# A streaming-encoder trunk on one core: the work beside the convolution's first block in another order

## The chip, the cores and the metric

The kernel runs on one core of a Trainium2 chip, as one program. The metric is its time on the device in microseconds (us), the median of several executions. PE is TensorE, DVE VectorE, ACT ScalarE, POOL GpSimd, SP SyncE, which here does nothing but start DMAs. Each engine takes its own instructions strictly in the order in which the program gives them to it, and waits for another engine's result where it needs one.

## The reference

Two layers work on 256 tokens of width 2048. The first mixes tokens with a convolution module, the second with latent attention, each followed by a squared-ReLU MLP; the edit lies in the convolution module and the norm ahead of it.

```python
def rms_norm(x, g):
    y = x * lax.rsqrt(jnp.mean(x * x, axis=-1, keepdims=True) + 1e-6)
    return y * g

def conv_module(h, w_pw1, b_pw1, w_dw, b_dw, ln_g, ln_b, w_pw2, b_pw2):
    u = h @ w_pw1 + b_pw1                     # 2048 -> 4096
    a, gate = jnp.split(u, 2, axis=-1)
    u = a * jax.nn.sigmoid(gate)
    u = lax.conv_general_dilated(u, w_dw, padding=[(30, 0)], ...) + b_dw   # 31 taps per channel
    u = jax.nn.silu(layer_norm(u, ln_g, ln_b))
    return u @ w_pw2 + b_pw2

x = x + conv_module(rms_norm(x, norm_mixer_g[0]), ...)
```

## The kernel before

Channels lie on the 128 partitions: h transposed is 16 chunks k of 128 channels by 256 tokens. The product with `w_pw1` and the convolution go through 16 blocks c of 128 channels. A block's product has two halves, the value and the gate, each a sum over the 16 chunks in a PSUM bank (`pss[c]`).

**The head.** Until the row sums of x are known, the norm's factor r isn't either. So x arrives in column parts, PE turns it chunk by chunk (`turn0`, L1048), and `gained(k)` takes the turned chunk from PSUM to `xg`, times the gain g (ACT L1053, DVE L1055). Block 0 is multiplied as plain fp32 from `xg`, without r (`first_products`, L1064). Then `rsqrt` gives r, PE turns it into a row (L1117), ACT copies that to SBUF (L1121), and for each pair p of chunks (8 pairs) three steps prepare the other blocks: `scaled(p)` multiplies the pair by r (DVE L1133), `upper(p)` rounds it to fp32r (ACT L1136), `lower(p)` subtracts the rounded from the unrounded (DVE L1139). Both parts are in `xt`, four tiles of two pairs each: `xt_96` has pairs 0 and 1, `xt_99` pairs 6 and 7. Block 0 gets its r behind the product, by two multiplications from PSUM (DVE L859).

**The weights.** A load n is 8 chunks of 256 columns (1 MB, in two DMAs of 512 KB, `conv_load`); load 2c + 0 or 1 belongs to block c. `conv_half(n, h)` splits one half of a load: ACT rounds (`hi`, L170), and GpSimd subtracts (`lo`, L174, 128x1024) for all loads of this stage. `conv_mm` (L837) then makes three products for each chunk and half: hi with upper, hi with lower, lo with upper. Block 1 reads load 2 with pairs 0 to 3, and load 3 with pairs 4 to 7.

**A block's round.** In round c, `glu(c - 1)` computes the sigmoid of the gate on ACT (`sg`, L861), the value plus its bias on ACT (`vb`, L870), and their product `ub`, on GpSimd (L871); for the last two blocks DVE does the latter two in one operation. `start_sum` begins two sums in PSUM with the first taps (ACT L901); one tap more is made on ACT for GpSimd (L876). `dve_taps` adds the others on DVE, one operation each (L931: `ub` from SBUF, the sum from PSUM), with the end of one block interleaved with the start of the next. PE meanwhile does `conv_mm(c)`, and later turns finished blocks for the layer norm's statistics (`to_tokens`, `ln_stats`), which need all blocks.

The order of the whole head is written out by hand (`manual_schedule`): an engine's order is the order of these calls in the program. Small vectors that the stage needs come as rows through seven DMAs on SP's queue (`stage_rows`, L307), and PE turns them (L312), as it turns the taps' weights (L1162), from where DVE copies them (L1165, L1166). In round 1 the pairs 6 and 7 are scaled, rounded and subtracted between `glu(0)` and the rounding of load 3's second half.

Of the kernel before, what the change touches and what calls it, by code (L numbers as in the profile page):

```python
# [10 lines left out]
F32 = mybir.dt.float32  # L11
# [3 lines left out]
AF = mybir.ActivationFunctionType  # L15
# [64 lines left out]
def trunk_kernel(  # L80
# [59 lines left out]
    def nm(s):  # L140
        uid[0] += 1
        return f"{s}_{uid[0]}"
# [615 lines left out]
    with ExitStack() as cx:  # L758
# [89 lines left out]
        def sum2_tile():  # L848
            return psum["sum"].tile([P, NB], F32, tag="sum2", name=nm("sum2"), bufs=1)

        def glu(c):
            ub = ubs[c] = branches[c % 3]
            sg = cv2.tile([P, S], F32, tag="sg", name=nm("sg"), bufs=1)
            va, ga = pss.pop(c)
            if c == 0:

                vb = cv2.tile([P, S], F32, tag="vb", name=nm("vb"), bufs=1)
                for o, ps in ((sg, ga), (vb, va)):
                    nc.vector.tensor_tensor(o, ps[:, :S], b2[:, :S], op=ALU.mult)  # L859
                va, ga = vb, sg  # L860
            nc.scalar.activation(sg, ga[:, :S], AF.Sigmoid, bias=b_pw1[:, KC + c : KC + c + 1])  # L861
            if c in (KC - 2, KC - 1):

                nc.vector.scalar_tensor_tensor(
                    out=ub[:, PAD:], in0=va[:, :S], scalar=b_pw1[:, c : c + 1], in1=sg, op0=ALU.add, op1=ALU.mult
                )
            else:
                if c > 0:
                    vb = cv2.tile([P, S], F32, tag="vb", name=nm("vb"), bufs=1)
                nc.scalar.activation(vb, va[:, :S], AF.Identity, bias=b_pw1[:, c : c + 1])  # L870
                nc.gpsimd.tensor_tensor(ub[:, PAD:], vb, sg, op=ALU.mult)  # L871

# [142 lines left out]
        with tc.manual_schedule():  # L1015
# [17 lines left out]
            def block_stats(n):  # L1033
                nc.vector.bn_stats(xst[:, n, :], xs[:, 0, n * NB : (n + 1) * NB])
# [11 lines left out]
            def turn0(ks, t):  # L1046
                for k in ks:
                    nc.tensor.transpose(where[k][:, t * P : (t + 1) * P], xs[:, t, k * P : (k + 1) * P], ident)  # L1048

            def gained(k, eng=nc.scalar):  # L1050
                g = g_mix[0][:, k : k + 1]
                if eng is nc.scalar:
                    nc.scalar.activation(xg[:, k, :], where[k], AF.Copy, scale=g)  # L1053
                else:
                    nc.vector.tensor_scalar(xg[:, k, :], where[k], scalar1=g, scalar2=None, op0=ALU.mult)  # L1055

            def first_products(*ks):


                order = [(k, b) for k in ks for b in range(2)]  # L1060
                if ks[-1] == KC - 1:
                    order.sort(key=lambda r: -r[1])
                for k, b in order:
                    nc.tensor.matmul(  # L1064
                        pss[0][b][:, :S], raws[k // 8][:, k % 8, b * P : (b + 1) * P], xg[:, k, :],
                        start=k == 0, stop=k == KC - 1,
                    )
# [12 lines left out]
            pss[0] = [acc_tile() for _ in range(2)]  # L1080

            gained(0)
            block_stats(2)
# [10 lines left out]
            turn0(range(8, 12), 1)  # L1094
            for p, tile_ in ((6, tr_tile), (7, sum_tile)):
                bank(p, tile_())
            turn0(range(12, 16), 0)
            first_products(2)
            turn0(range(12, 16), 1)
            first_products(3)  # L1100
# [10 lines left out]
            gained(4)  # L1111
            gained(5)
            for k in (6, 7):
                gained(k, nc.vector)
# [6 lines left out]
            nc.scalar.activation(r_row, r_ps[:, :S], AF.Copy)  # L1121
# [6 lines left out]
            def part(p, i):  # L1128
                return xt[p // 2][:, p % 2 * 2 : p % 2 * 2 + 2, i * S : (i + 1) * S]

            def scaled(p):
                row = r_row.rearrange("p (a n) -> p a n", a=1).broadcast_to([P, 2, S])
                nc.vector.tensor_tensor(pair(xr, p), pair(xg, p), row, op=ALU.mult)  # L1133

            def upper(p):
                nc.scalar.activation(part(p, 0), pair(xr, p), AF.Copy)  # L1136

            def lower(p):
                nc.vector.tensor_tensor(part(p, 1), pair(xr, p), part(p, 0).bitcast(F32), op=ALU.subtract)  # L1139

            first_products(4, 5)
            scaled(0)
            upper(0)
            for p in range(4):
                for k in (8 + 2 * p, 9 + 2 * p):
                    gained(k)
                scaled(p + 1)
                upper(p + 1)
                lower(p)
                first_products(6 + 2 * p, 7 + 2 * p)  # L1150
                if p == 0:
                    conv_load(3)
                if p in (1, 3):
                    conv_half(2, p // 2)
            scaled(5)
            upper(5)
            warm(AF.Sigmoid)
            lower(4)
            vt, wt = sum2_tile(), tr_tile()
            turn(n_vecs2, vecs2_rows, vt)  # L1160
            for j in range(4):
                nc.tensor.transpose(wt[:, j * NW : (j + 1) * NW], w_rows[j][:NW, :], ident[:NW, :NW])  # L1162
            first_products(14, 15)
            lower(5)
            nc.vector.tensor_copy(vecs[:, n_vecs:], vt[:, :n_vecs2])  # L1165
            nc.vector.tensor_copy(w_dw, wt[:, : 4 * NW])  # L1166
            conv_load(4)
            for c in range(1, KC + 1):
                n = UC * c
                conv_load(n + 3)  # L1170
                if c == 4:
                    nc.sync.dma_start(b2, conv_b_pw2[0:1, :].partition_broadcast(P))
                    nc.scalar.dma_start(pos_i, positions[0].rearrange("(t p) -> p t", p=P))
                    nc.scalar.dma_start(fr, inv_freq[0:1, :].partition_broadcast(P))
                glu(c - 1)
                if c == 1:
                    for p in (6, 7):
                        scaled(p)
                        upper(p)
                    conv_half(3, 0)  # L1180
                    for p in (6, 7):
                        lower(p)
# [791 lines left out]
```

## Time and profile before

| | us |
|---|---|
| median of 3 runs | 1937.01 |
| lowest and highest | 1936.37, 1937.33 |
| profiled execution | 1938.44 |
| span of its profile | 1936.7 |
| mean granted TensorE clock | 0.998 |
| PE, DVE, ACT, POOL busy | 1921.3, 1593.7, 1095.4, 240.9 |

A row of the timeline gives the start of an operation and its length in us, then engine, line, operation, the tiles written and read, partitions by elements, and how many are joined in the row; in brackets stands the idle time of the engine ahead of it and whose end came last before it began. In a row of windows, each engine has its busy time within the stretch and the number of its instructions. In the chain of waits each row is a piece of the time to the end, put down to what ran or was waited for.

### The profile page before, as it was taken

The numbers are of one execution on the slowest core, as the hardware profiler recorded it, in microseconds if no ns is written. First come the engines' busy times: TensorE is split into PE (matmuls) and PEld (weight loads), VectorE is DVE, ScalarE is ACT, GpSimd is POOL, SyncE is SP. The second block draws the span as 40 slices with busy tenths as digits, with TensorE's granted clock in tenths as the row PEclk, the third lists the DMA queues.
The fourth block names the chain that finished last, engine by engine and source line by source line (L and its number), as shares of the span: only waits on it lengthen the run. The fifth ranks groups of instructions, "written<-read, shape, count | busy, mean of one in ns | idle before, by whom it ended". The sixth has DMA issues, their size and how long they took to land.

```text
span 1936.7 us, 28367 instructions
## 1 busy us (share of the span) xinstructions
PE 1921.3 (99%) x10673; PEld 1680.6 (87%) x10673; DVE 1593.7 (82%) x2450; ACT 1095.4 (57%) x1643; POOL 240.9 (12%) x205
## 2 busy tenths in 40 slices
PE   8999999999999999999999999999999999999998
PEld 7999888888888888888898998888888888888886
DVE  6999989867999776799976765877789987778897
ACT  5557755555555555555576655555555554455554
POOL 4999200000010100000001420000000010000000
PEclk9999999999999999999999999999999999999999
DMA  7666456656576866546556445565546776665774
GB/s 224 197 190 181 154 194 213 186 189 196 173 235 211 250 196 196 187 171 204 204 180 185 141 132 184 164 212 184 191 160 224 218 248 220 193 195 175 231 221 145
DMA packets 230458, 375.48 MB, mean 194 GB/s; under 512 B 16424, under 2 KB 107824, under 8 KB 230064
## 3 DMA queue, kind: packets, MB, share of 16 engines
q1 hardware_dynamic: 224672, 363.28, 58.4%
q0 software_dynamic: 4320, 7.87, 2.2%
q10 hardware_dynamic: 1328, 2.52, 0.4%
q8 instruction: 83, 1.36, 0.3%
q14 instruction: 55, 0.45, 0.1%
HBM read 363.68 MB, written 2.10 MB: 189 GB/s over the span
## 4 chain that ended last, share of the span: by engine, by line
PE 96%; DVE 2%; DMA 1%; ACT 0%; issue 0%; SPq 0%; POOL 0%; ACTq 0%; DVEq 0%
PE acc L655 24%; PE acc L205 15%; PE acc L204 15%; PE acc L203 15%; PE acc L656 13%; PE acc L837 7%; PE acc L1317 2%; DVE sum L931 1%; PE acc L1565 0%; DMA raw<-in_conv_w_pw 0%; PE acc L1596 0%; PE acc L1595 0%; PE acc L1594 0%; PE acc L1566 0%; PE acc L1567 0%; DMA xs<-in_x 0%
## 5 line engine op out<-in xcount | busy, mean ns | idle before, releaser
L174 DVE TENSOR_TENSOR lo<-raw,hi 128x1024 fp32r<-128x1024 f32 (+2 forms) x509 | 602.0, 1197 | 231.5 <-ACT hi L170 224.7
L170 ACT ACTIVATE hi<-raw 128x1024 fp32r<-128x1024 f32 (+2 forms) x570 | 579.7, 1035 | 363.2 <-PE acc L655 203.0
L655 PE MATMUL acc<-xt,hi 128*128 128x512 f32 x2048 | 710.6, 390 | 0.0
L656 PE MATMUL acc<-xt,lo 128*128 128x256 f32 x2048 | 577.5, 282 | 0.0
L655 PEld LDWEIGHTS acc<-xt,hi 128*128 128x128 f32 x2048 | 384.5, 188 | 80.7
L656 PEld LDWEIGHTS acc<-xt,lo 128*128 128x128 f32 x2048 | 387.1, 189 | 0.2
L497 ACT ACTIVATE hi<-raw 128x1024 fp32r<-128x1024 f32 x248 | 228.6, 948 | 230.3 <-DVE raw L505 133.4
L498 DVE TENSOR_TENSOR lo<-raw,hi 128x1024 fp32r<-128x1024 f32 x248 | 263.9, 1087 | 29.4 <-ACT hi L497 25.2
L203 PE MATMUL acc<-hi,sh 128*128 128x512 f32 x514 | 200.1, 389 | 0.0
L205 PE MATMUL acc<-lo,sh 128*128 128x512 f32 x514 | 200.0, 389 | 0.0
L203 PE MATMUL acc<-hi,gh 128*128 128x512 f32 (+1 forms) x516 | 200.0, 388 | 0.0
L205 PE MATMUL acc<-lo,gh 128*128 128x512 f32 (+1 forms) x516 | 199.9, 387 | 0.0
L204 PE MATMUL acc<-hi,gl 128*128 128x512 f32 (+1 forms) x516 | 199.9, 387 | 0.0
L204 PE MATMUL acc<-hi,sl 128*128 128x512 f32 x450 | 175.1, 389 | 0.0
L837 PE MATMUL acc<-xt,hi 128*128 128x256 f32 x960 | 171.7, 282 | 0.3 <-ACT hi L170 0.3
L578 POOL DMA_DIRECT2D xs<-v x30 | 26.4, 976 | 1137.7 <-DVE lo L174 703.3
L931 DVE SCALAR_TENSOR_TENSOR sum<-ub,w_dw,sum 128x256 f32<-128x256 f32 x409 | 164.1, 482 | 2.7 <-ACT sum L901 2.2
L174 POOL TENSOR_TENSOR lo<-raw,hi 128x1024 fp32r<-128x1024 f32 x61 | 145.8, 2410 | 27.3 <-DMA stage<-in_conv_b_dw 20.6
L837 PEld LDWEIGHTS acc<-xt,hi 128*128 128x128 f32 x960 | 147.4, 190 | 0.6 <-ACT hi L170 0.5
L837 PE MATMUL acc<-xt,lo 128*128 128x256 f32 x480 | 134.8, 281 | 1.9 <-POOL lo L174 1.9
L203 PEld LDWEIGHTS acc<-hi,gh 128*128 128x128 f32 x516 | 96.9, 188 | 19.9
L204 PEld LDWEIGHTS acc<-hi,gl 128*128 128x128 f32 x516 | 96.9, 188 | 19.8
(313 smaller groups left out, 2555.0 us busy)
## 6 DMA issues: line engine op xcount, KB each, us to landing
raw<-in_mlp_w SPq DMA_DIRECT2D x255, 1024.0 KB, 5.4
raw<-in_conv_w_pw SPq DMA_DIRECT2D x62, 512.0 KB, 5.1
raw<-in_conv_w_pw SPq DMA_DIRECT2D x16, 1024.0 KB, 5.0
raw<-in_mla_w_o SPq DMA_DIRECT2D x16, 1024.0 KB, 5.3
raw<-in_mla_w_kv_up SPq DMA_DIRECT2D x32, 256.0 KB, 3.8
xs<-v POOLq DMA_DIRECT2D x30, 256.0 KB, 7.8
raw<-in_mla_w_in SPq DMA_DIRECT2D x8, 576.0 KB, 3.7
raw<-in_mla_w_in SPq DMA_DIRECT2D x4, 1024.0 KB
```

Source lines behind the costliest of these rows:

```text
L170: nc.scalar.activation(hi, raw[:, js, :], AF.Copy)
L174: eng.tensor_tensor(lo, raw, hi.bitcast(F32), op=ALU.subtract)
L203: nc.tensor.matmul(ps, sh, mh, start=start, stop=False)
L204: nc.tensor.matmul(ps, sl, mh, start=False, stop=False)
L205: nc.tensor.matmul(ps, sh, ml, start=False, stop=stop)
L497: nc.scalar.activation(hi, src, AF.Copy)
L498: nc.vector.tensor_tensor(lo, src, hi.bitcast(F32), op=ALU.subtract)
L655: nc.tensor.matmul(ps[b], wh[:, bs], xhl(k), start=k == 0, stop=False)
L656: nc.tensor.matmul(ps[b][:, :S], wl[:, bs], xh(k), start=False, stop=k == KC - 1)
L837: nc.tensor.matmul(pss[c][b][:, :S], w[i][:, bs], (xh, xl)[j](k), start=k == i + j == 0, stop=end and k == k0 + nk - 1 and (i, j) == terms ...
L931: nc.vector.scalar_tensor_tensor(out=out, in0=ubs[c][:, w : w + S], scalar=tap(c, w), in1=base, op0=ALU.mult, op1=ALU.add)
L1317: nc.tensor.matmul(ps2[b][t], x_kt(k, t), w[:, bs], start=k == g == i == 0, stop=k == KC - 1 and i == len(group) - 1,)
```

## The change

Five things are done, all in the head and in rounds 1 and the `glu` of block 0.

- PE: products of chunks 0 and 1 come ahead of the turns of chunks 8 to 11 of token half 0, product 2 ahead of the turns of half 1, product 3 ahead of the last turns. Later products also move up in the text, past scalings and splits, which on PE's own order changes nothing.
- `scaled(0)` reads r from PSUM, the copy comes behind it. `scaled(5)` and `scaled(6)` are done by GpSimd. Gains 10 and 13 go to DVE, 6 and 7 to ACT.
- The split of load 2 (both halves) comes behind the copy `upper(4)`; before, its halves stood behind `upper(2)` and `upper(4)`.
- `ub` of block 0 is made by DVE in one operation from `vb`, its bias and `sg`; ACT's `vb` and GpSimd's product go. `lower(5)` comes between the multiplications L859 and this product.
- `upper` and `lower` of pairs 6 and 7 go from ahead of load 3's first half and the sums to behind the sums and load 3's second half, directly ahead of the taps.

```diff
-        def glu(c):
+        def glu(c, between=None):
...
             nc.scalar.activation(sg, ga[:, :S], AF.Sigmoid, bias=b_pw1[:, KC + c : KC + c + 1])
-            if c in (KC - 2, KC - 1):
+            if c == 0:
+                between()
+            if c in (0, KC - 2, KC - 1):
                 nc.vector.scalar_tensor_tensor(
                     out=ub[:, PAD:], in0=va[:, :S], scalar=b_pw1[:, c : c + 1], in1=sg, op0=ALU.add, op1=ALU.mult
                 )
...
+            first_products(0, 1)
+            block_stats(2)
             turn0(range(8, 12), 0)
-            first_products(0, 1)
+            first_products(2)
             block_stats(3)
...
-            def scaled(p):
-                row = r_row.rearrange("p (a n) -> p a n", a=1).broadcast_to([P, 2, S])
-                nc.vector.tensor_tensor(pair(xr, p), pair(xg, p), row, op=ALU.mult)
+            def scaled(p, eng=nc.vector):
+                row = (r_ps[:, :S] if p == 0 else r_row).rearrange("p (a n) -> p a n", a=1).broadcast_to([P, 2, S])
+                eng.tensor_tensor(pair(xr, p), pair(xg, p), row, op=ALU.mult)
...
+            scaled(0)
+            nc.scalar.activation(r_row, r_ps[:, :S], AF.Copy)
...
+            scaled(2)
+            upper(1)
+            scaled(5, nc.gpsimd)
+            first_products(8, 9)
+            lower(1)
...
+            scaled(3)
+            upper(2)
+            scaled(6, nc.gpsimd)
...
+            scaled(4)
+            upper(3)
+            lower(3)
+            upper(4)
+            first_products(12, 13)
             vt, wt = sum2_tile(), tr_tile()
             turn(n_vecs2, vecs2_rows, vt)
...
+            lower(4)
+            conv_half(2, 0)
+            conv_half(2, 1)
+            scaled(7)
+            upper(5)
+            warm(AF.Sigmoid)
             first_products(14, 15)
-            lower(5)
...
-                glu(c - 1)
+                glu(c - 1, lambda: lower(5))
                 if c == 1:
-                    for p in (6, 7):
-                        scaled(p)
-                        upper(p)
                     conv_half(3, 0)
-                    for p in (6, 7):
-                        lower(p)
...
                 side_sum(c - 1)
+                if c == 1:
+                    for p in (6, 7):
+                        upper(p)
+                        lower(p)
                 dve_taps(c - 1)
```

DVE's order from the subtractions of pairs 4 and 5 to the first taps. A number behind a tile's name is its buffer; `ub_129` is the block that the taps read. Before:

```order
L1133 TENSOR_TENSOR xn<-xg,b_125 128x512
L1139 TENSOR_TENSOR xt_98<-xn,xt_98 128x2x256 x2
L1165 COPY vecs<-sum_40_332 128x120
L1166 COPY w_dw<-tr_333 128x496
L859 TENSOR_TENSOR sg_352<-acc_208,b_125 128x256
L859 TENSOR_TENSOR vb_353<-acc_207,b_125 128x256
L1133 TENSOR_TENSOR xn<-xg,b_125 128x512 x2
L1139 TENSOR_TENSOR xt_99<-xn,xt_99 128x2x256 x2
L931 SCALAR_TENSOR_TENSOR sum_371<-ub_129,w_dw,sum_371 128x256
```

DVE's order in the same place now:

```order
L1138 TENSOR_TENSOR xt_98<-xn,xt_98 128x2x256
L1132 TENSOR_TENSOR xn<-xg,b_125 128x512
L1182 COPY vecs<-sum_35_321 128x120
L1183 COPY w_dw<-tr_322 128x496
L859 TENSOR_TENSOR sg_353<-acc_208,b_125 128x256
L859 TENSOR_TENSOR vb_354<-acc_207,b_125 128x256
L1138 TENSOR_TENSOR xt_98<-xn,xt_98 128x2x256
L866 SCALAR_TENSOR_TENSOR ub_129<-vb_354,vecs,sg_353 128x256
L1138 TENSOR_TENSOR xt_99<-xn,xt_99 128x2x256 x2
L932 SCALAR_TENSOR_TENSOR sum_366<-ub_129,w_dw,sum_366 128x256
```

The second subtraction into `xt_98`, `lower(5)`, now stands behind the two multiplications L859; `ub` follows it on DVE, and the scalings of pairs 6 and 7 are gone from between.

GpSimd's order from its first work on data to block 1's `ub` (`ub_130`). Before:

```order
L174 TENSOR_TENSOR lo_302<-raw_140,hi_301 128x1024
L174 TENSOR_TENSOR lo_324<-raw_140,hi_323 128x1024
L871 TENSOR_TENSOR ub_129<-vb_353,sg_352 128x256
L174 TENSOR_TENSOR lo_364<-raw_289,hi_363 128x1024
L174 TENSOR_TENSOR lo_378<-raw_289,hi_377 128x1024
L174 TENSOR_TENSOR lo_457<-raw_346,hi_456 128x1024
L174 TENSOR_TENSOR lo_461<-raw_346,hi_460 128x1024
L871 TENSOR_TENSOR ub_130<-vb_517,sg_515 128x256
```

GpSimd's order now:

```order
L1132 TENSOR_TENSOR xn<-xg,b_125 128x512 x2
L174 TENSOR_TENSOR lo_330<-raw_140,hi_329 128x1024
L174 TENSOR_TENSOR lo_334<-raw_140,hi_333 128x1024
L174 TENSOR_TENSOR lo_361<-raw_287,hi_360 128x1024
L174 TENSOR_TENSOR lo_373<-raw_287,hi_372 128x1024
L174 TENSOR_TENSOR lo_456<-raw_347,hi_455 128x1024
L174 TENSOR_TENSOR lo_460<-raw_347,hi_459 128x1024
L872 TENSOR_TENSOR ub_130<-vb_516,sg_514 128x256
```

Two scalings came ahead of the splits, and the product for block 0 left from between them.

ACT's order from the copy of pair 4 on. Before:

```order
L1136 ACTIVATE xt_98<-xn 128x2x256
L170 ACTIVATE hi_323<-raw_140 128x1024
L1136 ACTIVATE xt_98<-xn 128x2x256
L244 ACT_TABLE_LOAD
L244 ACTIVATE warm_329<-ident 128x1
L861 ACTIVATE sg_352<-sg_352,vecs 128x256
L870 ACTIVATE vb_353<-vb_353,vecs 128x256
L1136 ACTIVATE xt_99<-xn 128x2x256 x2
L170 ACTIVATE hi_363<-raw_289 128x1024
L901 ACTIVATE sum_371<-ub_129,vecs,w_dw 128x256
L901 ACTIVATE sum_51_372<-ub_129,w_dw 128x256
L876 ACTIVATE tp_375<-ub_129,w_dw 128x256
```

ACT's order now, from the two halves of load 2 on:

```order
L170 ACTIVATE hi_329<-raw_140 128x1024
L170 ACTIVATE hi_333<-raw_140 128x1024
L1135 ACTIVATE xt_98<-xn 128x2x256
L244 ACT_TABLE_LOAD
L244 ACTIVATE warm_339<-ident 128x1
L861 ACTIVATE sg_353<-sg_353,vecs 128x256
L170 ACTIVATE hi_360<-raw_287 128x1024
L902 ACTIVATE sum_366<-ub_129,vecs,w_dw 128x256
L902 ACTIVATE sum_51_367<-ub_129,w_dw 128x256
L877 ACTIVATE tp_370<-ub_129,w_dw 128x256
L170 ACTIVATE hi_372<-raw_287 128x1024
L1135 ACTIVATE xt_99<-xn 128x2x256 x2
```

Both roundings of load 2 now stand together behind the copy of pair 4, and the copies of pairs 6 and 7 (`xt_99`) have gone from ahead of load 3 and the sums to behind them.

More of the change, by code (lines that the diff above doesn't have):

```diff
@@ L867, in glu @@
             else:
-                if c > 0:
-                    vb = cv2.tile([P, S], F32, tag="vb", name=nm("vb"), bufs=1)
+                vb = cv2.tile([P, S], F32, tag="vb", name=nm("vb"), bufs=1)
                 nc.scalar.activation(vb, va[:, :S], AF.Identity, bias=b_pw1[:, c : c + 1])
@@ L1082, in trunk_kernel @@
             gained(0)
-            block_stats(2)
             gained(1, nc.vector)
@@ L1094, in trunk_kernel @@
             turn0(range(8, 12), 1)
+            for k in (4, 5, 6):
+                gained(k)
             for p, tile_ in ((6, tr_tile), (7, sum_tile)):
@@ L1097, in trunk_kernel @@
             turn0(range(12, 16), 0)
-            first_products(2)
+            first_products(3)
             turn0(range(12, 16), 1)
-            first_products(3)
             nc.vector.tensor_tensor(xsq[:, 0:1], xsq[:, 0:1], xsq[:, 2:3], op=ALU.add)
@@ L1110, in trunk_kernel @@
             r0 = rsqrt(ms0, T, EPS, "n")
[L1111 to L1114, printed above, removed]
+            gained(7)
             r_ps = sum_tile()
@@ L1120, in trunk_kernel @@
             r_row = b2[:, :S]
-            nc.scalar.activation(r_row, r_ps[:, :S], AF.Copy)
             vecs2_rows = stage_rows(cv, vec_rows2, nc.sync)
@@ L1139, in lower @@
                 nc.vector.tensor_tensor(part(p, 1), pair(xr, p), part(p, 0).bitcast(F32), op=ALU.subtract)
+            scaled(0)
+            nc.scalar.activation(r_row, r_ps[:, :S], AF.Copy)
+            gained(8)
+            gained(9)
             first_products(4, 5)
-            scaled(0)
+            scaled(1)
             upper(0)
[L1144 to L1148, printed above, removed]
-                lower(p)
[L1150 to L1158, printed above, removed]
+            first_products(6, 7)
+            conv_load(3)
+            lower(0)
+            gained(10, nc.vector)
+            gained(11)
+            scaled(2)
[3 more added lines that the diff above has]
+            lower(1)
+            gained(13, nc.vector)
+            gained(12)
+            scaled(3)
+            upper(2)
+            scaled(6, nc.gpsimd)
+            first_products(10, 11)
+            lower(2)
+            gained(14)
+            gained(15)
+            scaled(4)
[3 more added lines that the diff above has]
+            first_products(12, 13)
             vt, wt = sum2_tile(), tr_tile()
@@ L1174, in trunk_kernel @@
                     nc.scalar.dma_start(fr, inv_freq[0:1, :].partition_broadcast(P))
-                glu(c - 1)
+                glu(c - 1, lambda: lower(5))
                 if c == 1:
-                    for p in (6, 7):
-                        scaled(p)
-                        upper(p)
                     conv_half(3, 0)
-                    for p in (6, 7):
-                        lower(p)
                 if c == KC:
```

## The prediction, made before the changed kernel ran

> **What bounds the kernel now.** I read the page first, then the chain of waits, then the head engine by engine.
>
> ```profile
> PE 1921.3 (99%) x10673; PEld 1680.6 (87%) x10673; DVE 1593.7 (82%) x2450; ACT 1095.4 (57%) x1643; POOL 240.9 (12%) x205
> PE 96%; DVE 2%; DMA 1%; ACT 0%; issue 0%; SPq 0%; POOL 0%; ACTq 0%; DVEq 0%
> ```
>
> TensorE is the bound of the kernel as a whole, but the edit touches only the head and the first block of the convolution, so the stage decides. Its windows (columns: PE, PEld, DVE, ACT, POOL busy, granted clock, DMA share, GB/s) and the end of its chain:
>
> ```profile
> 36.00:40.00 4.00, 4.00 (x23) 4.00 (x23) 4.00 (x11) 1.39 (x2) 4.00 (x2) 0.57 0.17 50
> 45.00:60.00 15.00, 15.00 (x131) 15.00 (x130) 15.00 (x39) 9.68 (x14) 14.72 (x9) 1.00 0.69 200
> 60.00:204.00 144.00, 144.00 (x1233) 143.72 (x1233) 143.18 (x365) 93.48 (x179) 137.28 (x78) 1.00 0.64 191
> 204.00:212.00 8.00, 7.67 (x42) 6.57 (x41) 7.76 (x24) 6.22 (x17) 4.67 (x7) 1.00 0.01 2
> ...
> 174.28 5.62 PE acc L837 x48
> 181.91 3.29 DVE sum L931 x9
> 203.77 4.47 DVE sum L931 x12
> 208.48 0.42 DVE ca L939
> ```
>
> From 45 us PE and DVE are both full: DVE's taps (L931) and PE's blocks (L837) keep the same pace, and the last 30 us of the stage's chain are DVE. From 45 to 212 DVE leaves 0.82 + 0.24 = 1.06 us empty. So the stage's end follows the start of the taps, less that 1.06 and less what DVE idles before 45. DVE there:
>
> ```profile
> 23.31 1.71 DVE L1139 TENSOR_TENSOR xt<-xn,xt 128x512 fp32r<-128x512 f32 x1 [2.80 <-ACT xt L1136]
> 24.95 0.68 DVE L1133 TENSOR_TENSOR xn<-xg,b 128x512 f32<-128x512 f32 x1
> 25.55 3.46 DVE L1139 TENSOR_TENSOR xt<-xn,xt 128x512 fp32r<-128x512 f32 x2
> 30.04 0.41 DVE L859 TENSOR_TENSOR vb<-acc,b 128x256 f32<-128x256 f32 x1
> 31.81 1.59 DVE L1139 TENSOR_TENSOR xt<-xn,xt 128x512 fp32r<-128x512 f32 x2 [0.16 <-ACT xt L1136]
> 33.75 8.72 DVE L931 SCALAR_TENSOR_TENSOR sum<-ub,w_dw,sum 128x256 f32<-128x256 f32 x22 [0.35 <-ACT sum L901]
> 44.98 1.27 DVE L931 SCALAR_TENSOR_TENSOR sum<-ub,w_dw,sum 128x256 f32<-128x256 f32 x3 [1.59 <-ACT sum L901]
> ```
>
> The taps begin at 33.75 and stop once, for 1.59 us, before 44.98. GpSimd beside them:
>
> ```profile
> 22.12 2.35 POOL L174 TENSOR_TENSOR lo<-raw,hi 128x1024 fp32r<-128x1024 f32 x1 [20.56 <-DMA stage<-in_conv_b_dw]
> 25.55 2.91 POOL L174 TENSOR_TENSOR lo<-raw,hi 128x1024 fp32r<-128x1024 f32 x1 [1.08 <-ACT hi L170]
> 31.13 1.12 POOL L871 TENSOR_TENSOR ub<-vb,sg 128x256 f32<-128x256 f32 x1 [2.68 <-ACT vb L870]
> 33.34 9.39 POOL L174 TENSOR_TENSOR lo<-raw,hi 128x1024 fp32r<-128x1024 f32 x4 [1.09 <-ACT hi L170]
> ```
>
> **The two exclude each other.** A subtraction L1139 costs about 0.69 us, ends of neighbours 0.6 apart; at 23.31 it took 1.71 and ended at 25.02, just behind GpSimd's split (22.12 + 2.35 = 24.47). At 25.55 DVE had two back to back: the first passed, GpSimd's split, asked for at the same moment, was stretched from 2.35 to 2.91, and the second subtraction ended at 29.01, behind the split's 28.46. So a DVE operation with both operands in SBUF and a GpSimd one hold each other up whole, and the one that waits goes next, even ahead of a back-to-back successor. Taps, with one operand in PSUM, run beside four splits at 33.34 (9.39/4 = 2.35 each) untouched.
>
> **PE in the head.**
>
> ```profile
> 9.23 0.66 PE L1048 MATMUL acc<-ident,xs 128*128 128x128 f32 x4 [1.17 <-DMA xs<-in_x]
> 22.45 1.99 PE L1064 MATMUL acc<-xg,raw 128*128 128x256 f32 x8 [0.66 <-ACT xg L1053]
> 24.96 0.29 PE L312 MATMUL sum<-ident,stage 120*128 120x120 f32 x1 [0.52 <-PE acc L1064]
> 25.52 1.90 PE L1064 MATMUL acc<-xg,raw 128*128 128x256 f32 x8
> 33.32 0.51 PE L837 MATMUL acc<-xt,hi 128*128 128x256 f32 x2 [0.31 <-ACT hi L170]
> 35.76 0.39 PE L837 MATMUL acc<-xt,lo 128*128 128x256 f32 x1 [1.93 <-POOL lo L174]
> ...
> 22.48 0.27 SPq L307 DMA_DIRECT2D stage<-in_mla_kv_norm_g x1
> ...
> L312 PEldq EVENT_SEMAPHORE  x4: 51/51/51, 24.4 to 24.9; - x4
> ```
>
> **The change part by part.**
>
> Products ahead of turns. This attacks the idle 1.17, 0.66 and 0.52. But the turn L312 needs the vector rows; the last is issued at 22.48, PE's sequencer works off its four waits until 24.9, and SP's order and issue times don't move. I keep L312 at 24.96; what PE wins ahead becomes idle there, about 2 us (the three sum to 2.35), worth 0. Bounds: if PE wasn't waiting for those rows, L312 comes up to 1.9 us sooner; if the clock is lowered behind that idle, products 14 and 15 (25.52 to 27.42) take longer. After the only idle of that size, 0.31 + 1.93 just before 35.76, the granted clock was 0.57.
> The Trainium skill (TensorE: Matmul & The Clock Gate, section "Why this matters for your kernels") allows gaps of up to about 3 us before the clock drops. The 0.57 above, behind 1.93 us, disagrees with it, so the measurement decides; by the page alone products 14 and 15 stay at full clock and the early case below gains weight, with its time of 1939.7.
>
> Scalings.
>
> ```profile
> 15.33 1.29 DVE L1133 TENSOR_TENSOR xn<-xg,b 128x512 f32<-128x512 f32 x2 [1.39 <-ACT b L1121]
> ```
>
> The first reads PSUM instead of waiting for ACT's copy of r; of the 1.39 that can give DVE about a microsecond. Pieces 5 and 6 on GpSimd cost there, by an estimate between a 128x256 product (1.12 with a wait in it) and 128x1024 (2.35), 1.3 each, and each holds up the subtraction that DVE asks for meanwhile by up to 1.3; I take 0.7. These cancel within some tenths: range -0.6 to +0.6 on what follows, by ACT's copies.
>
> Weights' split behind copies. ACT's rows:
>
> ```profile
> 23.89 0.64 ACT L1136 ACTIVATE xt<-xn 128x512 fp32r<-128x512 f32 x1
> 33.17 0.55 ACT L901 ACTIVATE sum<-ub,vecs,w_dw 128x256 f32<-128x256 f32 x1
> 34.46 2.93 ACT L170 ACTIVATE hi<-raw 128x1024 fp32r<-128x1024 f32 x3
> 43.06 0.47 ACT L870 ACTIVATE vb<-acc,vecs 128x256 f32<-128x256 f32 x1 [0.93 <-PE acc L837]
> ```
>
> Both halves of n=2 now come behind the copy of piece 4, here at 23.89. Kept there, the rounding starts at 24.5, takes 0.95 (three in 2.93), and GpSimd's two splits run about 25.5 to 27.9 and 27.9 to 30.2, the first copy perhaps some tenths earlier. Before, the first had passed by 24.47. PE's block 1 asks for the first at 27.06: up to 0.8 us of idle, hidden because DVE is later still.
>
> Now DVE. L859 reads block 0 when its last product ends, 27.42, and gives vb by about 27.8. Behind it on DVE stands lower(5), and behind that the product ub (now on DVE, both operands in SBUF), two more subtractions and all taps. lower(5) asks at 27.7 to 27.8, within 0.2 us of the moment at which GpSimd passes from one split to the next. With products 14 and 15 a little late, or the copies a little early, it misses. I take the miss:
> lower(5) waits to 30.2 and ends 30.9; GpSimd's third split, waiting, takes 30.8 to 33.1; ub is done at 33.4. Before it was 31.13 + 1.12 = 32.25.
>
> Then the sums L901 (33.40), the product for GpSimd and the rounding of n=3's second half on ACT, which in the rows above go from 33.17 to 34.46 and on by 0.98: 1.29 + 0.95, so ACT reaches the copy of piece 6 at 35.65. Before, copies 6 and 7 and both subtractions stood ahead of the sums, under no split. Now GpSimd starts its fourth split at 35.7, ahead of lower(6), which asks at 36.2 and gets through at 38.0 to 38.6. The fifth split, waiting, takes 38.6 to 40.85; lower(7) follows and the taps start at 35.7 + 2.3 + 0.55 + 2.3 + 0.55 = **41.4, 7.65 later**. ub itself is hidden there: the sums are ready at 34.4, the taps stand behind lower(7).
>
> PE's block 1 needs lower(6) and lower(7) for its last eighths, so it idles about 1 to 2 us twice near 38.5 and 41; in exchange its old idle 0.31 + 1.93 and its slow stretch go. Its end, at 43.06 before by ACT's wait, stays near 43, ahead of DVE: no further cost. If that cover went, up to 2 us.
>
> Sum: 7.65, less the 1.59 idle that has no reason left, less the 1.06 of slack (all of it, since a late DVE is what the rounds then wait for): +5.0; with no slack recovered +6.1. After the stage all is PE's chain, moved as a whole. The profiled execution (span 1936.7) would become 1941.7; it stands at 1938.44 with what lies around it, the median of the runs at 1937.01. I add to the median: **1942.0**.
>
> **The rivals.**
>
> Early: lower(5) asks in time and passes at 27.9 between the first two splits. For it: 0.2 us either way, and an earlier L312. Then ub waits once (to 31.05) and the rest repeats 2.33 sooner: taps at 39.07, 5.3 late, end +5.3 - 1.59 - 1.06 = +2.7, so 1939.7; with little slack recovered +3.7.
>
> DVE first: it keeps its place with lower(6) and lower(7) back to back. Against it: 25.55, where GpSimd went between two. For it: that is one instance. Saves 2.3: 39.1 after the miss, 36.8 after the early pass; +2.7 to +0.5, so about 1938.5.
>
> No waiting (the other side): the subtractions meet no split, since splits start later than I place them, and the order does what it says. Then ub is done at 29.2, ACT copies 6 and 7 by 33, the taps start at 33.3. Gain 0.45 + 1.59, and up to 1.06 of slack: -2.0 to -3.1, about 1935. PE would allow it: its idle of 0.31 + 1.93 goes, and from 36 to 40 it lost 0.43 x 4 = 1.7 by the clock. It decides if three of four meetings are avoided; the four splits from 33.34 to 42.7, back to back and moved by 2 us at most, speak against it.
>
> **How the numbers follow.** Chances: forecast 0.50, early 0.25, DVE first 0.09, no waiting 0.12, something unseen in PE's head that gives more 0.04. This kernel's measurement tells 0.2%, 3.9 us, from no change. Slower takes the forecast and a fifth of early, 0.55; faster needs more than the -3.1 of no waiting, 0.04 of it and the unseen 0.04: 0.08; same is the rest, 0.37. The range goes from 1937.5 (DVE first at its low end, +0.5) to 1944.4: +6.1, and 1.3 more in case the runs, unlike the profiled execution, seldom had the slow clock at 36 us whose loss the change trades in. The forecast's own range is 1941 to 1944.4.
>
> **What would show it.** DVE's taps begin at 41 (39 if early, 33 to 34 if nothing waits); lower(5), ub, lower(6) and lower(7) with spans of 2 to 3 us and ends just behind a GpSimd split; PE idle of about 2 us before L312 and before the last products of block 1; the layer norm's statistics some 5 us later. I am wrong if the subtractions keep 0.69 us beside the splits, if L312 moves forward by over a microsecond, or if DVE shows idle between 45 and 204 that lets a late start be made up.

## The result, and the profile after

| | median, us | lowest to highest | executions |
|---|---|---|---|
| before | 1936.32 | 1935.62 to 1938.16 | 9 |
| the change | 1941.26 | 1940.39 to 1942.58 | 9 |

The ratio is 1.0025, 95% interval 1.0014 to 1.0035: the change is slower, by 2.7 to 6.8 us. In the profiled execution (1941.32, span 1939.5) the chain of waits, by engine and by line, reads:

```profile
PE 89%; DVE 10%; ACT 1%; issue 1%; DMA 0%; DVEq 0%; ACTq 0%
PE acc L655 24%; PE acc L205 15%; PE acc L203 15%; PE acc L204 15%; PE acc L656 13%; DVE sum L932 8%; PE acc L1333 2%; PE acc L1581 0%; PE acc L1610 0%; PE acc L1612 0%; PE acc L1583 0%; PE acc L1582 0%; PE acc L1611 0%; PE tr L267 0%; PE a
```

Before, PE had 96% and DVE 2%. The convolution's blocks on PE (L837, 7% before) are gone from the chain; in their place stand 8% of DVE's taps (L932, L931 before). So the stage is now DVE's from the first tap to the last. The timeline of DVE:

```profile
27.35 1.41 DVE L1138 TENSOR_TENSOR xt<-xn,xt 128x512 fp32r<-128x512 f32 x1
29.04 2.27 DVE L866 SCALAR_TENSOR_TENSOR ub<-vb,vecs,sg 128x256 f32<-128x256 f32 x1 [0.28 <-ACT sg L861]
34.25 5.26 DVE L1138 TENSOR_TENSOR xt<-xn,xt 128x512 fp32r<-128x512 f32 x2 [2.94 <-ACT xt L1135]
39.43 8.71 DVE L932 SCALAR_TENSOR_TENSOR sum<-ub,w_dw,sum 128x256 f32<-128x256 f32 x22
...
214.22 0.49 DVE L1252 BATCH_NORM_AGGREGATE mv<-stats 128x2 f32<-128x33 f32 x2
```

lower(5) took 1.41, ub 2.27, lower(6) and lower(7) 5.26 together, where a subtraction alone takes 0.69. The taps start at 39.43. GpSimd in the same time, one row for the first scaling and two for six splits back to back:

```profile
18.73 1.27 POOL L1132 TENSOR_TENSOR xn<-xg,b 128x512 f32<-128x512 f32 x1 [17.16 <-ACT xg L1054]
25.70 7.89 POOL L174 TENSOR_TENSOR lo<-raw,hi 128x1024 fp32r<-128x1024 f32 x3 [2.90 <-ACT hi L170]
33.78 7.99 POOL L174 TENSOR_TENSOR lo<-raw,hi 128x1024 fp32r<-128x1024 f32 x3 [0.19 <-ACT hi L170]
```

But for 0.19 us, GpSimd runs without a pause from 25.70 to 41.8, and each of the four DVE operations named above, all with two operands in SBUF, falls into that time. PE, and SP's last vector row:

```profile
21.05 0.29 SPq L307 DMA_DIRECT2D stage<-in_mla_kv_norm_g  x1
...
23.33 0.27 PE L312 MATMUL sum<-ident,stage 120*128 120x120 f32 x1
23.86 1.90 PE L1065 MATMUL acc<-xg,raw 128*128 128x256 f32 x8
28.27 0.39 PE L837 MATMUL acc<-xt,lo 128*128 128x256 f32 x1 [2.10 <-POOL lo L174]
39.56 0.38 PE L837 MATMUL acc<-xt,hi 128*128 128x256 f32 x1 [1.79 <-DVE xt L1138]
```

The turn L312 came 1.6 us sooner than in the profile of before: SP issued the row 1.4 sooner, with SP's order unchanged, and PE didn't have to wait for it. What PE won went into 2.10 us of waiting for the first split. The windows (columns as before the change):

```profile
36.00:40.00 4.00, 2.21 (x17) 1.90 (x16) 4.00 (x4) 0.64 (x1) 4.00 (x3) 1.00 0.61 174
45.00:60.00 15.00, 12.62 (x106) 12.21 (x105) 14.96 (x40) 6.23 (x10) 10.82 (x7) 1.00 0.42 121
60.00:204.00 144.00, 144.00 (x1236) 143.93 (x1235) 143.72 (x369) 97.69 (x182) 137.18 (x79) 1.00 0.65 191
```

DVE has 0.04 + 0.28 us empty from 45 to 204, against 0.82 before: it sets the pace, and PE (12.62 of 15) waits for it.

### The profile page after: what moved, and what is told of

Same layout as the page of the kernel before. It is cut to its first block, busy times and chain, and to the rows that moved or that the text cites. A ratio compares the mean times of both kernels' runs of the same rounds, so it can differ in the third digit from the quotient of the medians.

```text
span 1939.5 us, 28369 instructions
## 1 busy us (share of the span) xinstructions
PE 1921.7 (99%) x10673; PEld 1680.2 (87%) x10673; DVE 1596.6 (82%) x2449; ACT 1095.4 (56%) x1642; POOL 243.5 (13%) x206
## 3 DMA queue, kind: packets, MB, share of 16 engines
q8 instruction: 83, 1.36, 0.3%
## 4 chain that ended last, share of the span: by engine, by line
PE 89%; DVE 10%; ACT 1%; issue 1%; DMA 0%; DVEq 0%; ACTq 0%
PE acc L655 24%; PE acc L205 15%; PE acc L203 15%; PE acc L204 15%; PE acc L656 13%; DVE sum L932 8%; PE acc L1333 2%; PE acc L1581 0%; PE acc L1610 0%; PE acc L1612 0%; PE acc L1583 0%; PE acc L1582 0%; PE acc L1611 0%; PE tr L267 0%; PE acc L1725 0%
## 5 line engine op out<-in xcount | busy, mean ns | idle before, releaser
L204 PE MATMUL acc<-hi,sl 128*128 128x512 f32 x450 | 175.1, 389 | 0.0
L837 PE MATMUL acc<-xt,hi 128*128 128x256 f32 x960 | 170.7, 281 | 2.2 <-DVE xt L1138 1.8
L932 DVE SCALAR_TENSOR_TENSOR sum<-ub,w_dw,sum 128x256 f32<-128x256 f32 x409 | 163.4, 485 | 0.3 <-ACT sum L902 0.2
L837 PEld LDWEIGHTS acc<-xt,hi 128*128 128x128 f32 x960 | 146.2, 188 | 3.0 <-DVE xt L1138 2.0
L837 PE MATMUL acc<-xt,lo 128*128 128x256 f32 x480 | 134.4, 280 | 4.1 <-POOL lo L174 4.1
L205 PEld LDWEIGHTS acc<-lo,sh 128*128 128x128 f32 x514 | 96.5, 188 | 20.6 <-DVE lo L498 0.4
```

The lines of the kernel that those rows point to most:

```text
L204: nc.tensor.matmul(ps, sl, mh, start=False, stop=False)
L205: nc.tensor.matmul(ps, sh, ml, start=False, stop=stop)
L837: nc.tensor.matmul(pss[c][b][:, :S], w[i][:, bs], (xh, xl)[j](k), start=k == i + j == 0, stop=end and k == k0 + nk - 1 and (i, j) == terms ...
L932: nc.vector.scalar_tensor_tensor(out=out, in0=ubs[c][:, w : w + S], scalar=tap(c, w), in1=base, op0=ALU.mult, op1=ALU.add)
```

## The experiments

Each was timed with the kernel before on the same chip. For each profile, the start of the first tap and of the layer norm's aggregation `mv` behind the last one (L1236 before) come from DVE's timeline; their difference is the stage as DVE sees it.

| kernel | median, us | ratio, interval | first tap | mv | difference |
|---|---|---|---|---|---|
| before, first profile | 1936.32 | | 33.75 | 211.65 | 177.90 |
| e1 before again | 1937.16 | 1.0001, 0.9992 to 1.0009 | 32.15 | 210.05 | 177.90 |
| the change | 1941.26 | 1.0025, 1.0014 to 1.0035 | 39.43 | 214.22 | 174.79 |
| e2 pairs back | 1939.53 | 1.0011, 1.0002 to 1.0020 | 37.36 | 212.13 | 174.77 |
| e3 split back | 1941.31 | 1.0023, 1.0014 to 1.0032 | 39.98 | 214.75 | 174.77 |
| e4 ub back | 1941.97 | 1.0025, 1.0015 to 1.0036 | 39.45 | 214.94 | 175.49 |
| e5 before, pairs late | 1941.35 | 1.0019, 1.0011 to 1.0028 | 38.89 | 213.84 | 174.95 |
| e6 pairs first | 1937.62 | 1.0002, 0.9993 to 1.0011 | 36.62 | 212.44 | 175.82 |
| e7 two splits on DVE | 1940.47 | 1.0019, 1.0011 to 1.0028 | 37.35 | 212.80 | 175.45 |
| e8 before, products first | 1937.13 | 1.0000, 0.9991 to 1.0009 | 32.34 | 210.25 | 177.91 |
| e9 scalings back | 1941.04 | 1.0020, 1.0012 to 1.0029 | 38.55 | 213.34 | 174.79 |
| e10 before, splits apart | 1933.96 | 0.9988, 0.9979 to 0.9997 | 32.01 | 206.78 | 174.77 |
| e11 before, third split on DVE, late | 1935.73 | 0.9995, 0.9986 to 1.0004 | 34.56 | 209.69 | 175.13 |
| e12 before, third split on DVE | 1934.87 | 0.9990, 0.9981 to 0.9999 | 32.92 | 207.99 | 175.07 |

The last column is 174.8 to 175.0 in the six profiles whose chain of waits runs through DVE's taps (the change, e2, e3, e5, e9, e10). In the other eight the chain runs for most of the stage through PE's blocks (L837), and the column is larger: 175.1 to 175.8, and 177.9 in the three where DVE waits before the second block's taps. So the stage ends with the later of two paths, the taps' start plus 174.8 or PE's blocks. In before it is PE's; the chain there goes from GpSimd's third split straight into block 1 on PE:

```profile
33.34 2.37 POOL lo L174
...
35.76 24.00 PE acc L837 x190
```

**e1: before again.** No edit.

> The kernel before, unchanged, profiled once more. Its nine runs have a median of 1936.3, the profiled one took 1938.4. Theory clock: the profiled execution paid 1.5 to 1.7 us for the slow clock behind PE's idle at 33.8 to 35.8 us, which most executions don't; then this profile shows a granted clock of 1.00 from 36 to 40, no DVE idle of 1.6 us before the second block's taps, and a span near 1935. Rival, SP: the profiled execution issued its DMAs late (the last vector row at 22.5 us, against 21.05 in the profile of the change); then this profile shows that row at 21 to 21.5 and everything behind it a microsecond earlier, with the slow clock or without.

DVE, SP, PE and the window of the slow clock in this second profile of before:

```profile
32.15 8.72 DVE L931 SCALAR_TENSOR_TENSOR sum<-ub,w_dw,sum 128x256 f32<-128x256 f32 x22 [0.35 <-ACT sum L901]
43.38 2.84 DVE L931 SCALAR_TENSOR_TENSOR sum<-ub,w_dw,sum 128x256 f32<-128x256 f32 x7 [1.59 <-ACT sum L901]
...
20.57 0.29 SPq L307 DMA_DIRECT2D stage<-in_mla_kv_norm_g  x1
...
23.52 0.27 PE L312 MATMUL sum<-ident,stage 120*128 120x120 f32 x1
34.16 0.39 PE L837 MATMUL acc<-xt,lo 128*128 128x256 f32 x1 [1.93 <-POOL lo L174]
...
36.00:40.00 4.00, 4.00 (x27) 4.00 (x26) 4.00 (x11) 0.00 (x0) 4.00 (x3) 0.71 0.49 138
```

The slow clock and DVE's idle of 1.59 are there again, so theory clock falls. The rival, SP, is right: the row went out at 20.57 instead of 22.48, and DVE's taps and `mv` stand 1.6 earlier. But the row only marks how late SP was. The chain of the first profile goes through another of SP's DMAs, one of weights, for which ACT waited ahead of its first rounding:

```profile
20.98 1.06 ACT L170 ACTIVATE hi<-raw 128x1024 fp32r<-128x1024 f32 x1 [1.80 <-DMA raw<-in_conv_w_pw]
```

SP issued that DMA at 13.48, in e1 at 12.40; there the same rounding starts at 19.23, without a wait.

The whole span shrank by 0.5 only; the other 1.1 went elsewhere and wasn't followed. The first profile of before was a late one: against this one, the change starts its taps 7.28 later, not 5.68, and has `mv` 4.17 later.

**e2, e3, e4, e9: the change less one part each.** Copies and subtractions of pairs 6 and 7 at their old place; load 2's first half split earlier; ub on ACT and GpSimd; both scalings on DVE.

```diff
                 if c == 1:                       # e2, and the lines behind side_sum removed
+                    for p in (6, 7):
+                        upper(p)
                     conv_half(3, 0)
+                    for p in (6, 7):
+                        lower(p)
...
             first_products(10, 11)               # e3
+            conv_half(2, 0)
...
-            conv_half(2, 0)
             conv_half(2, 1)
...
-            if c in (0, KC - 2, KC - 1):         # e4
+            if c in (KC - 2, KC - 1):
...
-            scaled(5, nc.gpsimd)                 # e9, and the same for 6
+            scaled(5)
```

> The change, but copies and subtractions of pairs 6 and 7 stand where they stood before, ahead of load 3's split and of the sums. Theory taps: the stage's end follows the start of DVE's taps (39.43 in the change), and the two subtractions that wait for a split each directly ahead of them (5.26 us in all) are most of the loss; expected: taps start at 32.6 to 37.1, depending on how many splits the subtractions still meet, and 2.3 to 5 us less than the change, 1936.3 to 1939. Rival, splits: the loss is PE's, which waits 2.10 us at 28.27 for load 2's split behind the copies; then this edit gives less than 1 us.

> The change, but load 2's first half is split behind the copy of pair 2 and GpSimd's second scaling, some 2 us earlier; the second half stays behind the copy of pair 4. Theory taps: lower(5) and ub meet one split less, taps start about 1.6 us earlier than 39.43, near 37.8, and the time falls by 1 to 2 us. Rival, splits: PE's idle of 2.10 at 28.27 goes and the time falls by 4 to 5 us, to that of before.

> The change, but the product ub of block 0 is made by ACT and GpSimd as before; lower(5) keeps its new place. Theory taps: ub stands behind the second split on GpSimd and is done at 31 to 31.5, as in the change where DVE waits for that same split (31.31); the third split starts 0.8 later. Within 1 us of the change, rather slower. Rival, ub: the product's move to DVE, with its 2.27 us there, is the loss; then 1.5 us or more come back.

> The change with its two scalings, of pairs 5 and 6, on DVE again. Theory pairs: the place of pairs 6 and 7 makes the loss, so it stays; without GpSimd's scalings two subtractions on DVE save their 0.66 of waiting each and pay 0.6 for each scaling, so the taps start within 1.2 us of 39.43 and the time is within 1 us of the change. Rival, GpSimd: the two scalings delay everything behind them, and 2 us or more come back.

DVE's rows, those of e2, then of e3, e4 and e9:

```profile
31.74 5.70 DVE L1138 TENSOR_TENSOR xt<-xn,xt 128x512 fp32r<-128x512 f32 x2
37.36 8.71 DVE L932 SCALAR_TENSOR_TENSOR sum<-ub,w_dw,sum 128x256 f32<-128x256 f32 x22
```

```profile
23.78 2.84 DVE L1132 TENSOR_TENSOR xn<-xg,b 128x512 f32<-128x512 f32 x1
39.98 6.35 DVE L932 SCALAR_TENSOR_TENSOR sum<-ub,w_dw,sum 128x256 f32<-128x256 f32 x16
```

```profile
34.33 5.20 DVE L1139 TENSOR_TENSOR xt<-xn,xt 128x512 fp32r<-128x512 f32 x2 [5.95 <-ACT xt L1136]
```

```profile
33.38 5.25 DVE L1138 TENSOR_TENSOR xt<-xn,xt 128x512 fp32r<-128x512 f32 x2 [2.94 <-ACT xt L1135]
```

e2 gives back 1.7 us by the medians, and 2.5 when each is taken against before beside it (2.46 over it, the change 4.94), near the least that was expected (2.3): even at the old place the subtractions meet two splits (5.70), since the splits of load 2 and load 3 now run where before GpSimd stood idle. e3 gives nothing, and both expectations miss: the earlier split meets the scaling of pair 4 (2.84 where one takes 0.69). In e4 and e9 the two subtractions keep their 5.2 and the time its loss, within 1 us of the change as expected. None of these four parts, taken out alone, brings the old time back.

**e5, e8: before with one part alone.** e5 has the pairs' copies and subtractions behind the sums and load 3's second half, e8 PE's products ahead of turns.

```diff
                     for p in (6, 7):             # e5
                         scaled(p)
-                        upper(p)
                     conv_half(3, 0)
-                    for p in (6, 7):
-                        lower(p)
...
                 side_sum(c - 1)
+                if c == 1:
+                    for p in (6, 7):
+                        upper(p)
+                        lower(p)
```

> The kernel before with one thing of the change alone: copies and subtractions of pairs 6 and 7 behind the sums and load 3's second half. Theory pairs: this place alone makes the loss, since each subtraction meets a split there; taps start at 38 to 40 (32.15 in the second profile of before), the two subtractions take some 5 us, and the time is that of the change, 4 us over before. Rival, sum of parts: e2 showed that taking this part out gives back only 1.7, so alone it costs about 2 and the other parts the rest.

> The kernel before with PE's part of the change alone: products 0 to 3 ahead of turns. Theory taps: block 0 is done sooner at most, but DVE reads it behind lower(4) and lower(5), so the taps start as before and the time stays within 1 us of before. Rival, PE: PE's idle in the head is on the path, and 1 to 2 us are won.

DVE and GpSimd of e5, then DVE of e8:

```profile
33.71 5.26 DVE L1139 TENSOR_TENSOR xt<-xn,xt 128x512 fp32r<-128x512 f32 x2 [3.54 <-ACT xt L1136]
38.89 7.53 DVE L931 SCALAR_TENSOR_TENSOR sum<-ub,w_dw,sum 128x256 f32<-128x256 f32 x19
...
30.73 10.47 POOL L174 TENSOR_TENSOR lo<-raw,hi 128x1024 fp32r<-128x1024 f32 x4
```

```profile
32.34 8.72 DVE L931 SCALAR_TENSOR_TENSOR sum<-ub,w_dw,sum 128x256 f32<-128x256 f32 x22 [0.35 <-ACT sum L901]
```

e5 alone has most of the loss, and by the intervals it may have all: 4.1 us over before beside it, against 4.9 for the change, with the same 5.26 and the taps at 38.89. The rival, a sum of parts in which this one costs about 2, falls: the parts don't add. The new place puts the subtractions beside splits; at the old place (e2) the change's later splits of load 2 and load 3 still meet them. e8 changes nothing: the taps start as in e1. By the order of DVE's instructions, it reads block 0 only behind its own subtractions, and this fits that.

**e6, e7: is it the meeting with the splits?** e6 exchanges two calls of the change; e7 has the fourth and fifth split subtracted by DVE.

```diff
                 if c == 1:                       # e6, and the same lines behind side_sum removed
+                    for p in (6, 7):
+                        upper(p)
+                        lower(p)
                     conv_half(n + 1, 1)
...
-                    conv_half(n + 1, 1)          # e7
+                    h31 = upper_half(raws[3], 1)
...
                     for p in (6, 7):
                         upper(p)
                         lower(p)
+                    wjs[3, 1] = lower_half(*h31, nc.vector)
+                    wjs[4, 0] = split_half(raws[4], 0, nc.vector)
...
+                if c == 1:
+                    conv_half(4, 1)
-                if c < KC - 1:
+                elif c < KC - 1:
                     conv_split(n + 2)
```

> The change with two calls exchanged: pairs 6 and 7 ahead of load 3's second half, both still behind the sums. Theory pairs: the fourth split then starts behind the subtractions instead of ahead of them; they meet at most the end of the third, taps start near 34.9 instead of 39.43, 4 us come back: 1936.5 to 1938. Rival, splits (PE): the fourth split comes a microsecond later on GpSimd, so PE waits longer and nothing is won.

> The change with the fourth and fifth split (load 3's second half, load 4's first) subtracted by DVE, behind lower(7), instead of by GpSimd. DVE has 2.3 us more work ahead of its taps. Theory port: with no GpSimd work beside them lower(6) and lower(7) take 1.3 us together instead of 5.26, so the taps start at about 37.8 although DVE does more, and the time falls by 1 to 2 us. Rival: the subtractions are slow there for another reason (their operands come late, or DVE itself); then they keep 5 us and the taps start at 41.7, 2 us slower.

PE and DVE of e6, then DVE and GpSimd of e7:

```profile
25.13 0.29 PE L312 MATMUL sum<-ident,stage 120*128 120x120 f32 x1 [1.89 <-DMA stage<-in_mla_kv_norm_g]
...
27.96 2.92 DVE L1138 TENSOR_TENSOR xt<-xn,xt 128x512 fp32r<-128x512 f32 x1
35.41 1.29 DVE L1138 TENSOR_TENSOR xt<-xn,xt 128x512 fp32r<-128x512 f32 x2 [2.00 <-ACT xt L1135]
36.62 8.71 DVE L932 SCALAR_TENSOR_TENSOR sum<-ub,w_dw,sum 128x256 f32<-128x256 f32 x22
```

```profile
33.87 1.29 DVE L1138 TENSOR_TENSOR xt<-xn,xt 128x512 fp32r<-128x512 f32 x2 [2.95 <-ACT xt L1135]
35.08 2.35 DVE L174 TENSOR_TENSOR lo<-raw,hi 128x1024 fp32r<-128x1024 f32 x2
...
25.30 7.89 POOL L174 TENSOR_TENSOR lo<-raw,hi 128x1024 fp32r<-128x1024 f32 x3 [2.90 <-ACT hi L170]
36.34 3.36 POOL L174 TENSOR_TENSOR lo<-raw,hi 128x1024 fp32r<-128x1024 f32 x1 [3.15 <-ACT hi L170]
```

With no split beside them (in e7 GpSimd stands idle from 33.19 to 36.34) the two subtractions take 1.29 in both, in e7 at the same place in DVE's order in which the change took 5.26. Theory port holds: DVE does 2.3 us more there and its taps still start 2.1 sooner. The time of e7 fell by 0.8 by the medians, a little under the 1 to 2 expected, and its interval and the change's overlap; `mv` comes 1.42 sooner, less than the taps, since most of e7's chain is PE's. e6 stands at 1.0002 of before, as expected, with nothing removed, only two calls exchanged.

The profile of e6 happens to be an execution with SP late (its taps start at 36.62, where 34.9 was expected): PE waits 1.89 for the last vector row, L312 stands at 25.13, and lower(5) then misses the gap between the first two splits (2.92). This is what the prediction assumed for the change; the change's own profile, with the row out at 21.05, shows lower(5) passing.

**e10, e11, e12: keeping splits and subtractions apart.** All three start from before. e12 rounds load 3's first half ahead of pairs 6 and 7 and subtracts it on DVE between scalings and subtractions. e10 adds that load 2's second half is rounded behind upper(5) and issued behind lower(4). e11 has products first, lower(5) behind the first glu, and load 3's first half subtracted by DVE behind lower(7).

```diff
                 if c == 1:                       # e12 and e10
+                    h30 = upper_half(raws[3], 0)
                     for p in (6, 7):
                         scaled(p)
                         upper(p)
-                    conv_half(3, 0)
+                    wjs[3, 0] = lower_half(*h30, nc.vector)
                     for p in (6, 7):
                         lower(p)
...
-                if p in (1, 3):                  # e10 alone
-                    conv_half(2, p // 2)
+                if p == 1:
+                    conv_half(2, 0)
             scaled(5)
             upper(5)
+            lower(4)
+            conv_half(2, 1)
             warm(AF.Sigmoid)
-            lower(4)
```

> The kernel before, with splits kept out of the subtractions' way: load 2's second half is rounded behind lower(4) and upper(5) in the text, ahead of the sigmoid's table load; load 3's first half is rounded ahead of pairs 6 and 7 and subtracted by DVE between their scalings and their subtractions. Theory: fewer meetings, and PE's idle of 1.93 us behind the third split shrinks, with the slow clock after it; taps start up to a microsecond later than 32.15, the 1.59 us of DVE idle goes: 1 to 2.5 us under before. Rival: DVE's 1.14 us more work and a start that is later eat it; within 1 us of before.

> The kernel before with PE's products ahead of turns, lower(5) behind the first glu's operations, and load 3's first half subtracted by DVE behind lower(7) instead of by GpSimd. Theory: as in the run before, the taps start near 32 to 33 and DVE doesn't idle at 43: 1 to 2.5 us under before. Rival: within 1 us of before.

> The faster of the last two runs with only one of its edits: load 3's first half rounded ahead of pairs 6 and 7 and subtracted by DVE between their scalings and subtractions; load 2's second half stays where before had it. Theory: this edit alone takes away PE's idle of 1.93 us at 34.16 and DVE's of 1.59 us at 43.38, so most of the 2.9 us is its; expected 1.5 to 2.5 us under before. Rival: without the other edit lower(4), lower(5) and the sigmoid stay late, the taps start a microsecond or more behind 32.15, and the time is within 1 us of before.

DVE, PE and the window of e10:

```profile
23.88 1.47 DVE L1139 TENSOR_TENSOR xt<-xn,xt 128x512 fp32r<-128x512 f32 x2
26.70 3.05 DVE L1133 TENSOR_TENSOR xn<-xg,b 128x512 f32<-128x512 f32 x2
29.67 1.21 DVE L174 TENSOR_TENSOR lo<-raw,hi 128x1024 fp32r<-128x1024 f32 x1
30.81 1.28 DVE L1139 TENSOR_TENSOR xt<-xn,xt 128x512 fp32r<-128x512 f32 x2
32.01 8.71 DVE L931 SCALAR_TENSOR_TENSOR sum<-ub,w_dw,sum 128x256 f32<-128x256 f32 x22
...
35.18 0.38 PE L837 MATMUL acc<-xt,lo 128*128 128x256 f32 x1 [0.69 <-POOL lo L174]
...
36.00:40.00 4.00, 4.00 (x37) 4.00 (x36) 4.00 (x12) 1.90 (x3) 4.00 (x3) 1.00 0.90 264
```

Although DVE does the 128x1024 subtraction itself (1.21), its taps start as early as in before, PE idles 0.69 instead of 1.93, the clock stays full from 36 to 40, and DVE doesn't run dry. e10 is faster than before by 0.03 to 0.21% (1933.96 against 1936.89 of before beside it, 2.9 us, where 1 to 2.5 was expected); e12 has 2.3 us (1934.87 against 1937.14), as expected, so the third split is most of it. e10 over e12 (0.9 us) can't be told from nothing by these intervals, nor e11 from before. e11's taps began at 34.56, not at 32 to 33; its profile is of its slowest execution (1937.10), and there the first scaling already stood 1.2 us behind e1's (16.66 against 15.50).

e12 shows the two paths apart. Its taps start 0.8 us later than in e1, yet `mv` comes 2.06 sooner, for its chain is PE's: PE waits 1.36 for a split instead of 0.18 and 1.93, and the first long stretch of L837 in the chain ends at 56.09 instead of 58.16, 2.07 sooner. In e10 PE is ahead, and the chain is the taps'. One profile each shows the clock, so how much the clock adds to DVE's saved idle wasn't separated.

## Why the prediction was right, and where not

- **What bounds the stage** held for the change, where the end follows the first tap. I took 1.59 + 1.06 = 2.65 us of room in before; the table shows 177.90 - 174.79 = 3.11. For before the step was incomplete: its chain is on PE's blocks from 35.76 to 179.90, so its end doesn't follow the taps, and the room is what DVE waits for PE.
- **DVE and GpSimd shut each other out** held, and e7 shows it with the splits beside the subtractions moved away: 1.29 against 5.26. The Trainium skill ("SBUF — State Buffer", section "Who interferes with whom") says that a VectorE instruction with two SBUF inputs contends with a GpSimd instruction that reads SBUF. Its section "SBUF: two separate sides" adds that whichever of the two starts first gets the shared ports for the whole instruction. These runs agree with both: the two take 1.29 alone, and in the change lower(6), asked for at 34.25 behind a split that began at 33.78, is held until that split is done.
- **lower(6) and lower(7)** were put at 36.2 to 41.4, 5.2 us; they took 5.26 from 34.25. e5 shows that this place alone makes most of the loss. The rival in which DVE keeps its place back to back was wrong in every profile with splits beside the two (5.20 to 5.70 in the change, e2, e3, e4, e5 and e9).
- **L312 kept at 24.96** failed, and by the prediction's own sign of being wrong: L312 moved forward by 1.6 us, more than the microsecond named there. I took the last row's issue time, 22.48, as fixed; SP's order is, its times aren't. The change's profile has 21.05 and L312 at 23.33, within the bound that the prediction gave (up to 1.9 sooner). In e6, with the row late, the assumed idle of 1.89 is there.
- **lower(5) misses** failed for the profiled execution: it passed between the splits, as the early rival has it, and the taps began at 39.43 where that rival has 39.07 and the forecast 41.4.
- **The size** came out near (1942.0 against 1941.26), but in part by luck: two offsets cancel. The taps start 2.0 earlier than forecast in the change, but also 1.6 earlier in before (32.15 in e1, 32.34 in e8) than in the one profile that the sum started from. So the delay is 7.28 instead of 7.65, with 3.11 of room instead of 2.65, and 4.17 at `mv`, against +5.0 forecast; what makes the medians differ by 4.94 and not 4.17 wasn't followed. The early rival's +2.7 is what the two first profiles alone show (214.22 - 211.65 = 2.57); against the runs it is too little.
- **PE** was expected idle near L312 and twice near 38 to 41. It idled 2.10 at 28.27 for the first split (0.8 was forecast, with L312 later) and 1.79 once. None of it was on the path, as said.
- **The clock** didn't drop behind the 2.10 us of idle in the change. The 1.3 us that the range held for runs without the slow clock at 36 us has no support in the profiles: e1 and e8 show it again (0.71 and 0.61).

## What to carry to other kernels

An order that reads better by engine can put two engines that share a port beside each other: look at what runs on GpSimd under each VectorE operation that takes both operands from SBUF, and count a meeting as up to the other's whole length (2.3 us here for an operation of 0.69). Moving one long operation to the engine that would otherwise wait for it can be cheaper than the wait (e10, e12), and exchanging two calls can be enough (e6). Before building a sum on absolute times of one profile, see how far a second execution of the same kernel moves them; here DMAs that SP issued late moved the stage by 1.6 us. Where two engines keep nearly the same pace, follow both: a delay on the one that isn't last is free up to the distance between them (3.11 us here), and a gain on it is worth nothing.

## What the hardware showed that was not expected

SP's issue times differ between executions of one program: the last of seven row DMAs went out at 22.48 and at 20.57 us in two profiles of before, and the taps moved by 1.6. The late profile's chain goes through a DMA of weights, issued at 13.48 instead of 12.40. Why SP was late wasn't tried.

The granted clock after an idle of PE isn't a matter of its length alone. Behind 1.93 us it was 0.57 and 0.71 over 36 to 40 us in the two profiles of before; behind 2.10 us, ended at 28.27 in the change, the next window shows 1.00:

```profile
28.00:32.00 4.00, 3.73 (x31) 3.73 (x32) 3.03 (x2) 2.60 (x6) 4.00 (x3) 1.00 0.74 224
```

Two idles of nearly the same length differ too: behind 1.80 us that ended at 39.02 in e5 the window from 40 to 45 shows 0.66, behind 1.79 that ended at 39.56 in the change it shows 1.00. What decides it wasn't tried.
